# Cutting the first load of a DMA-bound loss kernel into halves on two queues

## The chip, the cores and the metric

The kernel runs on one core of a Trainium2 chip. The time is that of the whole program on the device in microseconds, the median of several executions. The profile is one execution; its span is some 1.8 us shorter than the time of the same run. All runs told of here were recorded as fast, at a granted clock of 1.0.

## The reference

Cross entropy with label smoothing over 256 rows of 32000 classes, in float32:

```python
def reference(logits, labels, smoothing):      # (256, 32000), (256,), 0.1
    log_probs = logits - np.max(logits, axis=-1, keepdims=True)
    log_probs = log_probs - np.log(np.sum(np.exp(log_probs), axis=-1, keepdims=True))
    smooth_targets = np.full((batch, num_classes), smoothing / num_classes)
    for i, label in enumerate(labels):
        smooth_targets[i, label] = 1.0 - smoothing + smoothing / num_classes
    return (-np.sum(smooth_targets * log_probs, axis=-1)).astype(np.float32)
```

Three things are needed of each row: the sum of the logits, the sum of their exponentials, and the one logit at the label. The logits are 32.77 MB, and each is read once.

## The kernel before

Each of the 128 partitions holds two rows. The first row comes in four loads of 8000 columns, the second in ten loads that shrink from 8000 to 832, so that little is left to do after the last byte. Wide loads share a ring of three buffers. VectorE sums the logits and ScalarE the exponentials, in pieces of up to 4000 columns.

```python
WIDTHS = (
    (8000, 8000, 8000, 8000),
    (8000, 6272, 4736, 3648, 2688, 2048, 1536, 1216, 1024, 832),
)
...
def _issue_first_transfers_at_start(nc):
    # the first DMA of the sync and of the scalar queue is moved ahead of the opening barrier
    main, body = nc.m.functions[0].blocks[:2]
    head, rest = list(main.instructions), list(body.instructions)
    for engine in (mybir.EngineType.SP, mybir.EngineType.Activation):
        at = next(i for i, ins in enumerate(rest)
                  if ins.engine == engine and ins.opcode == "DMACopy")
        ...
        head.insert(to, rest.pop(at))
...
    lab = small.tile([P, 2 * R], I32, name="lab", tag="lab")
    nc.scalar.dma_start(out=lab[:], in_=labels...)      # 16 bytes a partition
    ...  # GpSimd: flat_idx = row offset + label, then two gathers of logits[flat_idx] into gat
...
    def load(w, col, name):
        if w >= RING_MIN:
            xt = ring.tile([P, max(WIDTHS[0])], FP32, name="xt", tag="xt")
        else:
            xt = tail.tile([P, w], FP32, name=name, tag=name)
        nc.sync.dma_start(out=xt[:, :w], in_=x[:, col : col + w])
        return xt
```

The softmax here doesn't subtract the row's maximum and nothing guards it: scores larger than these inputs give would overflow.

## Time and profile before

| | before |
|---|---|
| time, median of 3 | 85.47 us (85.46 to 85.61) |
| span of the profiled run | 83.6 us |
| DMA, mean over the span | 392 GB/s |
| ScalarE busy, VectorE busy | 72%, 47% |
| labels, issue to landing | 12.2 us |

No engine is at its limit over the whole span, and yet the transfers run without a break from 1 us to 78.7 us. Read the chain of waits first, then the times at which each new tile is first used. The prediction below shows both. ("L181 ACT ja" is ScalarE's exponential, "L169 DVE jd" VectorE's sum; q1 is the sync queue, q10 the scalar queue, q0 the pool queue.)

### The profile page before, as it was taken

To read this page: it belongs to the slowest core of one execution; us is meant where nothing else is said; L and a number is where in the kernel's file an instruction comes from. 1 tells how busy PE (TensorE), PEld (TensorE's weight loads), DVE (VectorE), ACT (ScalarE), POOL (GpSimd) and SP (SyncE) were. 2 spreads that over 40 slices of the span, in tenths; PEclk is the share of its full clock that TensorE was granted. 3 is DMA by queue.
4 is the path that set the end of the run, shared out by engine and by line. 5 is a ranking of instruction groups with operands and counts; after the bars stand their busy time and mean duration, and the time that the engine had idled before them with its cause. 6 is when DMAs were issued, how large, how long until landed. Compare 5 with 4: busy or idle time off the path is not lost.

```text
span 83.6 us, 214 instructions
## 1 busy us (share of the span) xinstructions
PE 1.5 (2%) x4; PEld 0.3 (0%) x4; DVE 38.9 (47%) x52; ACT 59.9 (72%) x45; POOL 7.1 (8%) x13
## 2 busy tenths in 40 slices
PE   0000000000000000000001010000000000000030
PEld 0000000000000000000000000000000000000000
DVE  0000019900595009910497119923936654756760
ACT  5000019992699809994499909998999999999950
POOL 2000009981010000000000000000000000000000
DMA  8979998999899989999999999999999999999400
GB/s 245 414 322 490 460 429 352 475 460 429 353 475 429 444 368 475 460 414 398 444 475 429 398 397 456 432 420 399 426 412 433 430 412 424 411 412 406 179 4 0
DMA packets 2227, 32.78 MB, mean 392 GB/s; under 512 B 433, under 2 KB 434, under 8 KB 946
## 3 DMA queue, kind: packets, MB, share of 16 engines
q1 hardware_dynamic: 2018, 32.77, 92.5%
q10 hardware_dynamic: 144, 0.00, 0.1%
q0 software_dynamic: 64, 0.00, 0.1%
q14 instruction: 1, 0.01, 0.0%
HBM read 32.77 MB, written 0.00 MB: 392 GB/s over the span
## 4 chain that ended last, share of the span: by engine, by line
DMA 84%; ACT 9%; DVE 2%; issue 1%; PE 0%; SPq 0%; DVEq 0%; ACTq 0%
DMA xt<-in_logits_dram 59%; DMA xl<-in_logits_dram 26%; ACT ja L181 9%; DVE jd L169 1%; PE lin_t L191 0%; SPq L163 0%; DVE lin_row L193 0%; DVE res L196 0%; DVE done L270 0%; DVEq L196 0%; DVEq L270 0%; ACTq L181 0%
## 5 line engine op out<-in xcount | busy, mean ns | idle before, releaser
L181 ACT ACTIVATE ja<-xt 128x4000 bf16<-128x4000 f32 (+1 forms) x12 | 40.9, 3408 | 19.4 <-DMA xt<-in_logits_dram 19.4
L169 DVE SCALAR_TENSOR_TENSOR jd<-xt 128x2000 f32<-128x2000 f32 (+1 forms) x12 | 26.1, 2176 | 31.4 <-DMA xt<-in_logits_dram 31.2
L181 ACT ACTIVATE ja<-xl 128x2368 bf16<-128x2368 f32 (+7 forms) x9 | 16.5, 1839 | 0.0
L169 DVE SCALAR_TENSOR_TENSOR jd<-xl 128x1184 f32<-128x1184 f32 (+7 forms) x9 | 10.7, 1184 | 7.3 <-DMA xl<-in_logits_dram 7.1
L123 POOL DMA_INDIRECT gat<-in_logits_dram,flat_idx x2 | 3.9, 1938 | 0.5 <-issue 0.3
L115 POOL TENSOR_TENSOR flat_idx<-rowoff,lab 128x2 int32<-128x2 int32 x1 | 2.0, 1999 | 11.1 <-DMA lab<-in_labels_dram 11.1
L181 ACT ACTIVATION_READ_ACCUMULATOR ja<-xt 128x1 f32 x12 | 2.2, 186 | 0.0
L90 ACT ACT_TABLE_LOAD x1 | 1.3, 1283 | 0.9 <-PEq L293 0.9
L181 ACT ACTIVATION_READ_ACCUMULATOR ja<-xl 128x1 f32 x9 | 1.6, 182 | 0.0
L191 PE MATMUL lin_t<-ident,both 128*1 128x128 f32 x1 | 0.4, 373 | 45.7 <-DVE both L218 45.7
L146 POOL TENSOR_SCALAR xsum<-gat 128x1 f32<-128x1 f32 x2 | 0.4, 214 | 7.3 <-DMA gat<-in_logits_dram,flat_idx 7.3
L193 DVE COPY lin_row<-lin_t 1x128 f32<-1x128 f32 x2 | 0.6, 280 | 0.9 <-PE lin_t L191 0.9
L169 DVE DVE_READ_ACCUMULATOR jd<-xt 128x1 f32 x12 | 1.0, 81 | 0.0
L196 DVE SCALAR_TENSOR_TENSOR res<-lin_row,lse_t 1x128 f32<-1x128 f32 x2 | 0.6, 276 | 0.8 <-PE lse_t L195 0.7
L191 PE MATMUL lin_t<-ident,done 128*1 128x128 f32 x1 | 0.4, 373 | 31.5 <-DVE done L270 31.5
L221 DVE TENSOR_REDUCE both<-esum 128x1 f32<-128x8 f32 x1 | 0.2, 161 | 1.6 <-ACT ja L181 1.6
L195 PE MATMUL lse_t<-ident,lse 128*1 128x128 f32 x2 | 0.7, 373 | 2.4 <-ACT lse L187 2.4
L169 DVE DVE_READ_ACCUMULATOR jd<-xl 128x1 f32 x9 | 0.7, 82 | 0.0
L270 DVE TENSOR_TENSOR done<-done,pair 128x2 f32<-128x2 f32 x2 | 0.3, 160 | 0.2
L189 ACT ACTIVATE lse<-elast,done 128x1 f32<-128x1 f32 x1 | 0.3, 261 | 0.2 <-DVE done L270 0.2
L187 ACT ACTIVATE lse<-both 128x1 f32<-128x1 f32 x1 | 0.2, 203 | 0.2 <-DVE both L221 0.2
masks.py:199 POOL TENSOR_SCALAR_AFFINE_SELECT ident<-ident 128x128 f32<-128x128 f32 x1 | 0.3, 282 | 0.0
(12 smaller groups left out, 1.6 us busy)
## 6 DMA issues: line engine op xcount, KB each, us to landing
xt<-in_logits_dram SPq DMA_DIRECT2D x5, 4000.0 KB, 21.4
xt<-in_logits_dram SPq DMA_DIRECT2D x1, 3136.0 KB, 19.2
xl<-in_logits_dram SPq DMA_DIRECT2D x1, 2368.0 KB
xl<-in_logits_dram SPq DMA_DIRECT2D x1, 1824.0 KB, 28.3
xl<-in_logits_dram SPq DMA_DIRECT2D x1, 1344.0 KB, 31.1
xl<-in_logits_dram SPq DMA_DIRECT2D x1, 1024.0 KB, 33.1
xl<-in_logits_dram SPq DMA_DIRECT2D x1, 768.0 KB, 34.4
xl<-in_logits_dram SPq DMA_DIRECT2D x1, 608.0 KB, 35.4
```

The costliest lines, as they stand in the source:

```text
L90: nc.scalar.add_instruction(mybir.InstLoadActFuncSet(name=nc.get_next_instruction_name(), act_func_set_id=tbl, ins=[], outs=[],))
L115: nc.gpsimd.tensor_tensor(out=flat_idx[:], in0=rowoff[:], in1=lab[:].rearrange("p (r two) -> p r two", two=2)[:, :, 0:1], op=ALU.add,)
L123: nc.gpsimd.indirect_dma_start(out=gat[:, r : r + 1], out_offset=None, in_=logits[:], in_offset=bass.IndirectOffsetOnAxis(ap=flat_idx[:, r ...
L146: nc.gpsimd.tensor_scalar(out=xsum[:, 0:1], in0=gat[:, r : r + 1], scalar1=label_weight, scalar2=None, op0=ALU.mult,)
L169: return nc.vector.scalar_tensor_tensor(out=jd[:, :h], in0=xp[:, :h], scalar=1.0, in1=xp[:, h:w], op0=ALU.mult, op1=ALU.add, accum_out=out,)
L181: nc.scalar.activation(out=ja[:, :w], in_=xp, func=AF.Exp, accum_out=out)
L189: nc.scalar.activation(out=lse[:], in_=se, func=AF.Ln, bias=se_rest)
L191: nc.tensor.transpose(out=lin_t[:], in_=lin, identity=ident[:])
L193: nc.vector.tensor_copy(out=lin_row[:], in_=lin_t[:])
L195: nc.tensor.transpose(out=lse_t[:], in_=lse[:], identity=ident[:])
L196: nc.vector.scalar_tensor_tensor(out=res[:, :, r : r + 1], in0=lin_row[:], scalar=-c_small, in1=lse_t[:], op0=ALU.mult, op1=ALU.add,)
L270: nc.vector.tensor_tensor(out=done[i + 1][:], in0=done[i][:], in1=pairs[i][:], op=ALU.add)
```

## The change

The first load has nothing before it to hide behind. The change wants it to start on two queues at once, both ahead of the opening barrier (where the engines wait for one another at the start; the first issue behind it comes at 0.92 us in the kernel before). The labels held the scalar queue's place there, so they move to the pool queue, behind the barrier.

```diff
-    nc.scalar.dma_start(
+    nc.gpsimd.dma_start(
         out=lab[:], in_=labels.bitcast(I32).rearrange("(p f) -> p f", p=P)
     )
@@ load()
-        nc.sync.dma_start(out=xt[:, :w], in_=x[:, col : col + w])
+        if col == 0:
+
+            h = w // 2
+            nc.sync.dma_start(out=xt[:, :h], in_=x[:, :h])
+            nc.scalar.dma_start(out=xt[:, h:w], in_=x[:, h:w])
+        else:
+            nc.sync.dma_start(out=xt[:, :w], in_=x[:, col : col + w])
```

## The prediction

> **What bounds the kernel now.** I read the page's chain of work first, because an average over the span cannot say which wait ends last.
>
> ```profile
> ## 4 chain that ended last, share of the span: by engine, by line
> DMA 84%; ACT 9%; DVE 2%; issue 1%; PE 0%; SPq 0%; DVEq 0%; ACTq 0%
> q1 hardware_dynamic: 2018, 32.77, 92.5%
> ```
>
> The last line is the sync queue in the table of queues: packets, MB, share of the 16 DMA engines' span. The chain is a chain of transfers, and one queue carries all the logits. So the question is whether that stream ever stops. The timeline answers with the times at which the first operation on each new tile starts (start, length, engine; in brackets the idle time ahead and what ended it):
>
> ```profile
> 12.14 3.54 ACT L181 ACTIVATE ja<-xt 128x4000 bf16<-128x4000 f32 x1 [9.94 <-DMA xt<-in_logits_dram]
> ...
> 21.70 3.54 ACT L181 ACTIVATE ja<-xt 128x4000 bf16<-128x4000 f32 x1 [2.41 <-DMA xt<-in_logits_dram]
> ...
> 31.35 3.54 ACT L181 ACTIVATE ja<-xt 128x4000 bf16<-128x4000 f32 x1 [2.50 <-DMA xt<-in_logits_dram]
> ...
> 40.84 3.54 ACT L181 ACTIVATE ja<-xt 128x4000 bf16<-128x4000 f32 x1 [2.34 <-DMA xt<-in_logits_dram]
> ```
>
> A tile of 128 x 8000 floats is 4.096 MB. The tiles come 9.56 us apart (21.70 - 12.14), which is 4.096 MB / 9.56 us = 428 GB/s, and that pace doesn't change. ScalarE waits 2.3 to 2.5 us for each tile, so compute is not the bound here. Buffers aren't either: the fourth load is issued at 19.3 us, when the first tile has been used, while the queue still holds tiles two and three. From 57.7 us on ScalarE is busy without a gap (22.32 us of 22.40), fitted to the shrinking tiles, and the last tile lands as ScalarE is free for it. Both clocks hang on the same stream: move it by d and the end moves by about d.
>
> What is left to gain lies ahead of the stream. The first tile is used at 12.14 us; less 9.56 us of transfer, 2.58 us are fixed: issue, first byte, a ramp and the landing. Here is the ramp, by narrow windows of the DMA view (0 to 1.0, 1.0 to 2.5 and 2.5 to 12.2 us):
>
> ```profile
> DMA packets 0, 0.00 MB, mean 0 GB/s; under 512 B 0, under 2 KB 0, under 8 KB 0
> ...
> q1 hardware_dynamic: 16, 0.51, 113.7%
> ...
> q1 hardware_dynamic: 144, 4.10, 98.5%
> q10 hardware_dynamic: 144, 0.00, 0.8%
> ```
>
> No packet starts in the first microsecond. Then each of the 16 engines starts one packet of 32000 bytes (0.51 MB / 16), a whole row of the tile. Narrower windows put 12 of those starts before 1.3 us and the last four between 1.4 and 2.2 us. All 16 packets of that window take 1.137 x 1.5 us x 16 / 16 = 1.7 us each; from 5 to 6 us one takes 1.185 x 1.0 x 16 / 16 = 1.185 us. So the first packet costs 0.5 us more than a later one. After 2.5 us the labels' packets (q10, the scalar queue) stand beside those of the tile.
>
> **What the Trainium skill says.** "DMA: Bandwidth & Descriptors", section "Queues, rings and completion order": each DMA engine takes turns between the queues it has work for, packet by packet. The trace agrees: from 5 to 6 us both queues have 16 packets, one of 16 bytes for each of 32000. It explains a label load of 2 KB that takes 12.2 us from issue to landing (8 packets on each engine, each waiting for a 1.19 us row), and it says how two halves will share the engines.
>
> The same page, section "Issuing engines are not separate DMA queues": starting transfers from several engines saves only the sequencer's time of issue. In this trace that is short: the first issue on the sync queue takes 0.40 us, the label issue on the scalar queue runs from 0.12 for 0.38 us. Whether two queues fill the ramp better, the trace before can't show.
>
> The same page, section "Latency and other measured facts": first byte some 600 ns after a hardware-generated issue, some 1 us on the GpSimd path. The trace: issue done at 0.40 us, first packet at 1.00 us, so 0.6 us; no such row exists for a direct GpSimd load.
>
> The same page, section "Where 436 GB/s comes from": a ceiling of 435 GB/s at the ports. The stream's 428 GB/s is 98% of it, so a second queue has no rate to find.
>
> **The change, part by part.**
>
> 1. Labels leave the scalar queue. Removed: one issue of 0.38 us on a queue whose next work (the table load) waits for the barrier until 0.91 us anyway; worth 0. Also removed are 144 small packets among the first tile's rows, 0.8% of 9.7 us x 16 engines, which is 0.08 us an engine. They would come back on the pool queue in fewer packets: the two gathers, 256 elements and 32 completions by their shape, show only 64 packets there. I keep 0.06 us of gain.
>
> 2. Labels on the pool queue. Issued after the barrier, at about 1 us, landing at 3 to 6 us in place of 12.3, as grouped packets need fewer turns (my estimate). The index addition and the gathers then begin 6 to 9 us sooner. What needs them is the reduction over the label terms, at 45.48 us, while the second label term is ready at 26.79 us: 18.7 us of slack before, more after. Worth 0.
>
> 3. The first load in halves. Each half has 128 rows of 16000 bytes, so 8 packets an engine on either queue, turn by turn. The data is the same and so is its rate. What is added: 128 row packets more (the rows are cut in two) and 16 completions. For the cost of a packet I compare sizes. From 77.8 to 78.6 us, 63 packets take 51.6%, 6.60 us; less 15 completions of 9 ns, 48 rows of 3328 bytes take 0.135 us each. The line through (3328 B, 0.135 us) and (32000 B, 1.185 us) has a slope of 27.3 GB/s an engine and an offset of 0.013 us. Eight more packets an engine: 8 x 0.013 = +0.10 us.
>
> 4. The start. The sync issue at 0 us still has 128 rows to describe, so the first packet still comes at 1.00 us. The scalar queue's half is issued at 0.12 us, where the labels were, and its packets can be there from about 1.1 us. For twelve engines nothing is won. The four late ones start 0.4 to 1.1 us behind; if it is the sync queue's descriptors that they lack, the other queue may feed them sooner. The tile is complete only when the slowest engine is done. I give this 0.2 us: a third of the late engines' lag of 0.6 us, as the lag may equally be HBM answering late (the late packets are the shorter ones, and end only some 0.4 us behind the rest).
>
> 5. When compute may start. Each half carries its own completion, and the first piece of 4000 columns is just the first half. As the queues take turns, both end together near 12 us, so the first piece starts at most a packet or so earlier. ScalarE then waits 2.4 us for tile two anyway: worth 0.
>
> Sum: -0.06 + 0.10 - 0.2 = -0.16 us; 85.47 - 0.16 = 85.31, which I round to 85.3 us.
>
> **The rivals.**
>
> Nothing moves at all. The late starts are HBM's, and the packet costs cancel: 85.4 to 85.5 us. For it: the late packets are short. Against it: little; it is nearly as likely as my own.
>
> The start is won in full. All engines begin at 1.0 us and the doubled supply hides part of the first packet's extra 0.5 us: 0.5 to 0.8 us less, 84.7 to 85.0 us. For it: 2.58 us are fixed, and two queues give an engine two packets to work on at once. Against it: the engine already had a queue of packets behind the first, and still showed the 0.5 us.
>
> The second half comes late. If the scalar queue starts later or is served less, the sync queue goes on with tile two, and the first tile is whole some time after 12.14 us. For it: nothing, as the labels got one turn in two. Against it: ScalarE's idle 2.4 us ahead of tile two takes up such a delay, and bytes are only reordered: within 0.1 us of 85.47.
>
> A new cost elsewhere. The pool load could hold up the barrier or slow the stream. Against it: it is issued after the barrier, and the gathers on the same queue passed beside the stream between 16 and 20 us without a change of the 9.56 us step. If wrong, 85.6 to 85.8 us.
>
> **Range and chances.** Most outcomes lie from the full start (84.9) to a small new cost (85.7); the runs before spread over 0.15 us. Two per cent are 1.71 us. To gain that, two thirds of the fixed 2.58 us would have to go; to lose it, the stream would have to stop for longer than a row's packet takes. I see no row for either: 2% each, and 96% for within 2%.
>
> **What would show each step.** Right: DMA packets start at about 1.0 us and carry 16000 bytes on both queues, in equal number, up to about 12 us; tile two is used 0 to 0.4 us before 21.70, and every later tile and the end by as much; the label load lands before 7 us and the gathers run before 12; the steps between tiles stay at 9.56 us. Step 4 is wrong if the first packets are as staggered as before, or if tile two comes more than 0.5 us sooner. Step 3 is wrong if tile two comes later than 21.70 us with the same start. The whole account is wrong if the steps between tiles change, if ScalarE waits for anything but a landing or its own work, or if the end moves by an amount other than tile two's.

## The result, and the profile after

| | before | after |
|---|---|---|
| time, median of 6 | 85.5 us (85.38 to 85.66) | 85.3 us (85.15 to 85.46) |
| ratio, 95% interval | | 0.9975 [0.9957, 0.9993] |
| span of the profiled run | 83.6 us | 83.5 us |

A ratio is the mean time of one kernel's fast runs over that of the other's in the same rounds, so not quite the ratio of the medians. The gain is 0.0025 x 85.5 = 0.21 us, with an interval of 0.06 to 0.37 us. It is clear of zero and small. The two profiled runs took 85.36 us (before) and 85.33 us (after), so they differ by far less than the gain.

The chain of waits after. Its tail now runs through ScalarE where it ran through the transfers:

```profile
## 4 chain that ended last, share of the span: by engine, by line
DMA 59%; ACT 34%; DVE 2%; issue 1%; PE 0%; SPq 0%; DVEq 0%; ACTq 0%
```

This is no new bottleneck. In both kernels ScalarE works without a gap from the first use of tile six on (57.77 us before, 57.70 us after), the last tiles land just about when it is free for them, and from there to the issue of the result the two take 23.63 and 23.68 us. The chain's share moves by 25 points while that stretch changes by 0.05 us.

The timeline after, with the first operation on each half of tile one and on tiles two to four (start, length, idle time ahead):

```profile
11.50 3.54 ACT L187 ACTIVATE ja<-xt 128x4000 bf16<-128x4000 f32 x1 [9.31 <-DMA xt<-in_logits_dram]
...
15.04 3.52 ACT L187 ACTIVATE ja<-xt 128x4000 bf16<-128x4000 f32 x1
...
21.73 3.54 ACT L187 ACTIVATE ja<-xt 128x4000 bf16<-128x4000 f32 x1 [3.07 <-DMA xt<-in_logits_dram]
...
31.27 3.54 ACT L187 ACTIVATE ja<-xt 128x4000 bf16<-128x4000 f32 x1 [2.40 <-DMA xt<-in_logits_dram]
...
40.76 3.54 ACT L187 ACTIVATE ja<-xt 128x4000 bf16<-128x4000 f32 x1 [2.33 <-DMA xt<-in_logits_dram]
```

Tile one is used 0.64 us sooner than before (11.50 against 12.14), but tile two comes at 21.73 in place of 21.70, tile three at 31.27 in place of 31.35. ScalarE spends the head start waiting: 3.07 us ahead of tile two, where it was 2.41. The result's transfer is issued at 81.38 us in place of 81.40. So this pair of profiles shows 0.02 us of the 0.21 at the end, and at most 0.08 on the way; the rest lies in how the runs spread.

The DMA issues after (KB, us from issue to landing):

```profile
xt<-in_logits_dram SPq DMA_DIRECT2D x1, 2000.0 KB, 11.5
xt<-in_logits_dram ACTq DMA_DIRECT2D x1, 2000.0 KB, 13.1
...
lab<-in_labels_dram POOLq DMA_DIRECT2D x1, 2.0 KB, 6.5
```

The halves don't land together: the scalar queue's, issued at 0.12 us, lands near 13.2 us, 1.7 us after the sync queue's. The first microseconds show when they start. ("Ramp" means here the stretch from the first packet until every engine keeps the steady pace.) The DMA view of the changed kernel from 1.0 to 2.8 us and from 2.8 to 3.0 us:

```profile
q1 hardware_dynamic: 32, 0.51, 98.4%
...
q10 hardware_dynamic: 9, 0.14, 172.1%
```

Before 2.8 us the scalar queue moves nothing. The sync queue's first 32 packets, two on each engine, are the same 0.51 MB that the kernel before moved as 16 whole rows by then. Only after them do the queues take turns. The second queue thus gave the ramp no byte more.

### The profile page after: what moved, and what is told of

Read it like the earlier page. It is cut to its first block, busy times and chain, and to the rows that moved or that the text cites. A ratio compares the mean times of both kernels' runs of the same rounds, so it can differ in the third digit from the quotient of the medians.

```text
span 83.5 us, 217 instructions
## 1 busy us (share of the span) xinstructions
PE 1.5 (2%) x4; PEld 0.3 (0%) x4; DVE 38.7 (46%) x52; ACT 59.9 (72%) x45; POOL 4.2 (5%) x14
## 4 chain that ended last, share of the span: by engine, by line
DMA 59%; ACT 34%; DVE 2%; issue 1%; PE 0%; SPq 0%; DVEq 0%; ACTq 0%
DMA xt<-in_logits_dram 59%; ACT ja L187 34%; DVE jd L175 1%; PE lin_t L197 0%; DVE done L276 0%; SPq L169 0%; DVE lin_row L199 0%; DVE res L202 0%; ACTq L187 0%; DVEq L202 0%; DVEq L276 0%
## 5 line engine op out<-in xcount | busy, mean ns | idle before, releaser
L123 POOL DMA_INDIRECT gat<-in_logits_dram,flat_idx x2 | 2.0, 1002 | 0.7 <-POOL ident masks.py:199 0.4
L103 POOL DMA_DIRECT2D lab<-in_labels_dram x1 | 0.8, 753 | 1.0 <-POOLq L299 1.0
L115 POOL TENSOR_TENSOR flat_idx<-rowoff,lab 128x2 int32<-128x2 int32 x1 | 0.2, 195 | 5.4 <-DMA lab<-in_labels_dram 5.4
## 6 DMA issues: line engine op xcount, KB each, us to landing
xt<-in_logits_dram SPq DMA_DIRECT2D x1, 2000.0 KB, 11.5
```

Source lines behind the costliest of these rows:

```text
L103: nc.gpsimd.dma_start(out=lab[:], in_=labels.bitcast(I32).rearrange("(p f) -> p f", p=P))
L123: nc.gpsimd.indirect_dma_start(out=gat[:, r : r + 1], out_offset=None, in_=logits[:], in_offset=bass.IndirectOffsetOnAxis(ap=flat_idx[:, r ...
```

## The experiments

Each kernel was run beside the kernel before on the same chip. All gave correct results. The first four shared one set of 11 runs of before (median 85.51 us), the next four one of 7 (85.34 us), the last four one of 11 (85.41 us). My theory was the prediction's sum: packets cost, the second queue's ramp gains. The first rival was that the labels' move is all of it, the second that nothing moves.

**The changed kernel once more.** No edit.

> The changed kernel once more, as the measure for the other three of this call. Theory (the prediction's sum): 0.16 us less than the kernel before, ratio 0.998. Rival (nothing moves): ratio 1.000 within 0.001. The profile should repeat what the first one showed: the first half used near 11.5 us, the second landing near 13.2 us, tile two used within 0.1 us of the 21.70 us of before.

Measured: 85.33 us, ratio 0.9969 [0.9935, 1.0003]. Tile one used at 11.56, tile two at 21.80, the scalar half landing 13.2 us after its issue. The wider interval comes from before, which ranged from 85.23 to 86.21 us, while the changed kernel stayed within 85.25 to 85.39. With the first result the gain is now measured twice at 0.2 to 0.3 us, though this second interval just reaches zero gain.

**Labels only.** The first load whole on the sync queue, nothing of the scalar queue ahead of the barrier:

```diff
-    for engine in (mybir.EngineType.SP, mybir.EngineType.Activation):
+    for engine in (mybir.EngineType.SP,):
-            nc.sync.dma_start(out=xt[:, :h], in_=x[:, :h])
-            nc.scalar.dma_start(out=xt[:, h:w], in_=x[:, h:w])
+            nc.sync.dma_start(out=xt[:, :w], in_=x[:, :w])
```

> Only the labels move to the pool queue; the first load stays whole on the sync queue. The prediction's sum gives this part -0.06 us, ratio 0.9993. Rival (all of the measured 0.2 us comes from taking the label packets out of the first tile's rows and the gathers to another time): ratio 0.9975, like the whole change. If the split is what gains, this one stays at 0.999 to 1.000.

> Labels on the pool queue and the first load whole, once more, as the intervals of the first four runs overlap. Prediction's sum: 0.9993. Labels are all of it: 0.9975 or lower, and below the split-only kernel of this call by 0.002.

Measured: 85.39 us, ratio 0.9978 [0.994, 1.0016]; and later 85.35 us, 0.9990 [0.9969, 1.0011]. Both intervals hold both expectations. The two profiles of this one kernel are worth more than its times. Tile two and the issue of the result, first in the profile of a run of 85.67 us:

```profile
22.17 3.54 ACT L185 ACTIVATE ja<-xt 128x4000 bf16<-128x4000 f32 x1 [2.72 <-DMA xt<-in_logits_dram]
...
81.81 0.32 SPq L278 DMA_DIRECT2D out_dram<-res  x1
```

then tile two in the profile of a run of 85.36 us:

```profile
21.91 3.54 ACT L185 ACTIVATE ja<-xt 128x4000 bf16<-128x4000 f32 x1 [2.54 <-DMA xt<-in_logits_dram]
```

The same program has tile two 0.26 us apart in two runs that are 0.31 us apart. They come from two chips, but on the first of them alone this kernel ranged from 85.17 to 85.74 us. Such differences in the first 20 us are as large as the whole effect, so no single pair of profiles can account for 0.2 us.

**Split only.** The labels stay on the scalar queue, behind the half; the half is the one that goes ahead of the barrier:

```diff
-    nc.gpsimd.dma_start(
+    nc.scalar.dma_start(
         out=lab[:], in_=labels...
-        at = next(
+        found = [
             i for i, ins in enumerate(rest)
             if ins.engine == engine and ins.opcode == "DMACopy"
-        )
+        ]
+        at = found[1 if engine == mybir.EngineType.Activation else 0]
```

> Only the split: halves on the sync and the scalar queue ahead of the barrier, the labels on the scalar queue behind the half. The prediction's sum gives +0.10 for the packets and -0.2 for the ramp, -0.10 us, ratio 0.9988. Rival (labels are all of it): ratio 1.000 or a little above (up to 1.001, for eight more packets an engine).

> Halves on two queues with the labels behind the half on the scalar queue, once more. Prediction's sum: 0.9988. Labels are all of it: 1.000 to 1.001, above the labels-only kernel of this call by 0.002.

Measured: 85.52 us, ratio 0.9994 [0.9957, 1.0031]; later 85.35 us, 0.9996 [0.9974, 1.0017]. Again both intervals hold both expectations, and the two parts differ by 0.0006 later, where "labels are all of it" asked for 0.002. The means of the two calls are 0.9984 for labels only, 0.9995 for split only and, with its first result, 0.9972 for the whole change. They lean towards the labels, but the difference of 0.0011 is 0.1 us, and each interval reaches 0.0021 or more to either side: the order of the two parts is not settled.

**Both halves on the sync queue.** The packets of the change, without its second queue. The second half is issued behind the barrier, at 0.80 us:

```diff
-    for engine in (mybir.EngineType.SP, mybir.EngineType.Activation):
+    for engine in (mybir.EngineType.SP,):
-            nc.scalar.dma_start(out=xt[:, h:w], in_=x[:, h:w])
+            nc.sync.dma_start(out=xt[:, h:w], in_=x[:, h:w])
```

> Both halves on the sync queue, the first ahead of the barrier, the second behind it; labels on the pool queue. It has the packets of the change without its second queue. The prediction's sum gives -0.06 + 0.10 = +0.04 us, ratio 1.0005. If the second queue is worth nothing (the changed profile shows its first packet only at 2.8 us, behind two packets of the sync queue), this one ties with the whole change, ratio 0.9975, and the first half is used some 5 us sooner, near 7.5 us, with no effect on the end.

> Both halves on the sync queue, labels on the pool queue, once more: it was the fastest of the first four. If the second queue gains nothing, again 0.996 to 0.998, no slower than the changed kernel's 0.9975; by the prediction's step 4 it should lack the 0.2 us of the ramp and stand at 1.0005.

Measured: 85.25 us, ratio 0.9963 [0.993, 0.9997]; later 85.22 us, 0.9985 [0.9959, 1.0011]. It is as fast as the changed kernel, with the lowest median. The later interval holds 1.0005 too, so by time it is the first that speaks: there the six runs of the changed kernel average 85.33 us and the six of this one 85.25, where step 4 had the second queue 0.2 us ahead. Its first profile: the DMA view from 1.0 to 2.8 us, then the first uses of the two halves and of tile two.

```profile
q1 hardware_dynamic: 33, 0.53, 101.4%
```

```profile
7.50 3.54 ACT L187 ACTIVATE ja<-xt 128x4000 bf16<-128x4000 f32 x1 [5.42 <-DMA xt<-in_logits_dram]
...
12.08 3.54 ACT L187 ACTIVATE ja<-xt 128x4000 bf16<-128x4000 f32 x1 [0.95 <-DMA xt<-in_logits_dram]
...
21.71 3.54 ACT L187 ACTIVATE ja<-xt 128x4000 bf16<-128x4000 f32 x1 [5.99 <-DMA xt<-in_logits_dram]
```

33 packets on one queue, where the two queues had 32 (all of them of the sync queue): the ramp is the same. The first half comes 4 us sooner than with two queues, and nothing comes of it: ScalarE waits 5.99 us for tile two, which is there at 21.71. The claim that the second queue gains 0.2 us in the ramp falls with this.

**The start behind the barrier.** This asks whether the end follows the stream at all:

```diff
-    nc.at_finalize(_issue_first_transfers_at_start)
```

> The changed kernel with both halves issued behind the opening barrier. Central claim (move the stream by d and the end moves by d): the first packet comes some 0.8 us later, at 1.8 us, tile two and the end by as much, so +0.6 us over before, ratio 1.007. If the end hangs on something else (ScalarE's tail), ratio under 1.002.

Measured: 86.29 us, ratio 1.0104 [1.0083, 1.0125]. From its timeline, the first issues, then tile two and the issue of the result:

```profile
0.73 0.40 SPq L165 DMA_DIRECT2D xt<-in_logits_dram  x1
0.76 0.39 ACTq L166 DMA_DIRECT2D xt<-in_logits_dram  x1
...
22.86 3.54 ACT L186 ACTIVATE ja<-xt 128x4000 bf16<-128x4000 f32 x1 [2.79 <-DMA xt<-in_logits_dram]
...
82.50 0.32 SPq L279 DMA_DIRECT2D out_dram<-res  x1
```

Against the changed kernel, tile two is 1.13 us later (22.86 - 21.73) and the result's issue 1.12 us (82.50 - 81.38). The end follows the stream one to one, as claimed. The size was off: the issue is 0.73 us later, as is the first packet (1.75 us in place of 1.0), and 0.4 us more is lost before tile two. Part of that can be chance, as the labels-only kernel showed; I have no run that splits it. One thing is different here: the scalar queue's packets start at 2.5 us, 1.3 us after its issue ends, and both halves land within 0.1 us of each other (0.73 + 12.2 and 0.76 + 12.3).

**The first tile on the scalar queue.** Why was that queue late? Here it is alone ahead of the barrier:

```diff
-    for engine in (mybir.EngineType.SP, mybir.EngineType.Activation):
+    for engine in (mybir.EngineType.Activation,):
-            nc.sync.dma_start(out=xt[:, :h], in_=x[:, :h])
-            nc.scalar.dma_start(out=xt[:, h:w], in_=x[:, h:w])
+            nc.scalar.dma_start(out=xt[:, :w], in_=x[:, :w])
```

> The first tile whole on the scalar queue ahead of the barrier, nothing of the sync queue ahead of it. Asks why the scalar queue's packets came only at 2.8 us. If that queue starts late by itself, its first packet stands near 2.6 us again, the sync queue's tile two goes first from some 1.7 us. If it was only behind the two packets that each engine had taken from the sync queue, its first packet stands near 1.0 us. Tile one then shares its turns with tile two and is used late, at 18 to 20 us; ScalarE has about 20 us to spare over the span but waits in the middle, so the time may rise by up to 3 us, ratio 1.00 to 1.04.

The DMA view from 0 to 1.4, from 1.4 to 5.0 and from 5.0 to 6.0 us:

```profile
q10 hardware_dynamic: 9, 0.29, 71.2%
...
q10 hardware_dynamic: 39, 1.25, 86.3%
...
q1 hardware_dynamic: 15, 0.28, 66.5%
```

Alone, the scalar queue starts between 1.0 and 1.2 us, as promptly as the sync queue did: it isn't late by itself. Now it is the sync queue that comes late: its first load is issued from 0.93 to 1.33 us and moves nothing until after 5 us, while each engine takes three rows from the scalar queue. So in both runs the queue that reached the idle engines first kept them to itself, for 1.8 us in the change and 4.1 us here. That settles which queue waits; why the wait lasts so long, no run shows. The time, 90.84 us (ratio 1.0647, beyond the 1.04 expected), says nothing on this: the program builder put one of the later, smaller loads (4736 columns) first on the sync queue, so the order of the loads differs.

**Rows cut in quarters.** The cost of a cut row, made large: the four other loads of 8000 columns come as four loads of 2000 each.

```diff
-            nc.sync.dma_start(out=xt[:, :w], in_=x[:, col : col + w])
+            q = w // 4 if w == max(WIDTHS[0]) else w
+            for o in range(0, w, q):
+                nc.sync.dma_start(out=xt[:, o : o + q], in_=x[:, col + o : col + o + q])
```

> The changed kernel with the other four loads of 8000 columns cut into quarters on the sync queue: 24 more row packets an engine for each of four tiles, 96 in all. The prediction's 0.013 us a packet gives +1.25 us over the changed kernel, so +1.05 us over before, ratio 1.012, and a step between tiles of 9.87 us in place of 9.56. If a cut row costs nothing beside its neighbours: as the changed kernel, ratio 0.9975, step 9.56.

Measured: 86.01 us, ratio 1.0080 [1.0063, 1.0097]. From its timeline, the second piece of tile two and of tile five:

```profile
26.74 3.54 ACT L191 ACTIVATE ja<-xt 128x4000 bf16<-128x4000 f32 x1 [1.15 <-DMA xt<-in_logits_dram]
...
50.93 3.54 ACT L191 ACTIVATE ja<-xt 128x4000 bf16<-128x4000 f32 x1 [1.20 <-DMA xt<-in_logits_dram]
```

ScalarE takes two pieces of a tile, and waits for a landing before each of the six from the first of these lines to the last: five half tiles, 24.19 us, 9.68 us a tile. With whole rows the steps from tile three to tile five in the changed kernel were (50.24 - 31.27) / 2 = 9.49 us. The 24 packets and three completions added cost 0.19 us, 7 ns each. By time: (1.0080 - 0.9972) x 85.34 = 0.92 us over 108 packets and completions, 8.5 ns each, or 6 to 11 ns with the intervals of both ratios (my estimate; the two come from different calls). The prediction's 13 ns, taken from a line through two packet sizes, was too much.

**Nine label loads.** The cost of small packets, made large: eight more loads of the labels behind the first in the kernel before, into tiles that nothing reads.

```diff
+    for j in range(8):
+        more = small.tile([P, 2 * R], I32, name=f"more{j}", tag=f"more{j}")
+        nc.scalar.dma_start(out=more[:], in_=labels...)
```

> The kernel before with eight more label loads on the scalar queue, into tiles that nothing reads: the cost of one label load beside the rows, times eight. The prediction's 0.08 us an engine for one load gives +0.64 us, ratio 1.0075. Rival (the label packets are all of the 0.2 us that the change gained, each turn costs more than its own 9 ns): +1.6 us, ratio 1.019. If small packets cost the stream nothing: ratio 1.000.

Measured: 88.62 us, ratio 1.0391 [1.0368, 1.0414], beyond every expectation. The waits of the sync queue name the cause:

```profile
SPq L168 <- DMA more<-in_labels_dram: 11.7, 1, 11.7
```

A logits load waited 11.7 us for one of the added label loads, with which it shares no data. The trace says why: its entry for each issue, which the views don't print, names the semaphore that the transfer counts up when it lands and the one that the issue waits for. In this run the loads on the sync and scalar queues take eight semaphores in turn, numbers 100 to 107. The second logits load has number 102, which the first added label load had before it; that one landed at 12.54 us, and the logits load was issued at 12.56. In the 40 slices of this run the rate falls to 6 GB/s at 10.8 us. The experiment shows what a starved stream costs, not what small packets cost.

**One transfer of small packets.** The same question with one more load, 64 runs of 16 bytes on each engine:

```diff
+    more = small.tile([P, 8, 8], FP32, name="more", tag="more")
+    nc.scalar.dma_start(
+        out=more[:, :, 0:4],
+        in_=x[:, 0:64].rearrange("p (j k) -> p j k", k=8)[:, :, 0:4],
+    )
```

> The eight extra label loads stopped the stream for another reason than their packets (the second logits load waited for one of them to land, a semaphore being used again), so the cost of small packets is asked again with one transfer: the kernel before with one more load on the scalar queue, 64 runs of 16 bytes an engine, into a tile that nothing reads. At the 9 ns that the trace shows for one, 64 x 9 ns = +0.58 us, ratio 1.007. Rival (the nine packets an engine of one label load are all of the 0.2 us gained, some 22 ns each): +1.4 us, ratio 1.017. If they cost nothing: 1.000.

Measured: 88.88 us, ratio 1.0401 [1.0373, 1.0428]. One waiting load spoiled this time too, but only near the end: the load of 2688 columns has the semaphore of the added load, which landed at 68.79 us, and was issued at 68.81. The sync queue's waits, and the rate in 40 slices of 2.2 us:

```profile
SPq L168 <- DMA more<-in_logits_dram: 28.5, 1, 28.5
```

```profile
GB/s 235 397 353 427 456 442 456 427 383 427 427 471 412 383 427 456 442 456 398 383 442 442 430 369 473 439 404 418 400 410 370 20 252 433 431 400 419 264 4 4
```

The hole is at slice 32 (67 to 70 us). Ahead of it the stretch is clean. From tile two to tile six every engine moves 32 rows, each with one small packet beside it, as the DMA view from 25 to 30 us shows (the first two lines are the kernel with the added load, the last is before):

```profile
q1 hardware_dynamic: 64, 2.05, 95.3%
q10 hardware_dynamic: 65, 0.00, 0.7%
```

```profile
q1 hardware_dynamic: 64, 2.05, 95.1%
```

Tile two to tile six take 58.54 - 22.15 = 36.39 us here and 57.77 - 21.70 = 36.07 us in the kernel before: 0.32 us for 32 small packets, 10 ns each. One label load, nine packets an engine, therefore costs 0.09 us. The rival that gives all of the gain to these packets, at 22 ns each, falls.

## Why the prediction was right

The predicted time was 85.3 us and the measured one is 85.3; the predicted change -0.16 us, the measured -0.21 with 0.06 to 0.37 as its interval. The frame held, but not all the terms.

- **The stream sets the end.** Right, and shown: with the start behind the barrier, a tile two later by 1.13 us gave an end later by 1.12. Two halves or one, an earlier first tile is worth nothing (7.50, 11.50 or 12.14 us, all with tile two near 21.7).
- **The step of 9.56 us "doesn't change".** Not quite: in the kernel before the steps between tiles are 9.56, 9.65 and 9.49 us. The slowest holds the gathers' packets, which run from 21.0 to 26.1 us and not, as the prediction read it, between 16 and 20 us, when only their instructions ran; after the change the packets run sooner and that step is 9.54.
- **Step 1, labels off the scalar queue.** Right in size: 0.08 us by its own working, 0.09 us by the added small packets. The set-off of 0.02 us for the pool queue was never timed by itself, but its packet count fits: that queue moves 96 packets after the change and 64 before, two more an engine.
- **Step 2, labels on the pool queue.** Worth nothing, as said. Its time was not: used at 8.07 us, where 3 to 6 us was the estimate and 7 us the mark. Its issue ends at 2.19 us and no packet of its queue starts before 5.8 us. Whether this is the wait behind another queue that the scalar queue met too, no run shows.
- **Step 3, cut rows.** The right sign, too large: 7 to 8.5 ns a packet, so 0.06 to 0.07 us in place of +0.10.
- **Step 4, the ramp.** This step failed. "Its packets can be there from about 1.1 us" is contradicted by the profile, which has none before 2.8 us, and the 0.2 us it was to gain can't come from there: on one queue the same halves give the same ramp and the same time. The trace before had the warning in it: the label load, issued at the same 0.12 us on the same queue, has no packet before 2.6 us (a window from 0 to 2.6 us shows q1 alone), and the prediction's own view from 1.0 to 2.5 us shows none of q10. (Also, of the four late first packets three are short; the one of 1.6 to 1.8 us took 1.79 us, more than the average of 1.7.)
- **Step 5, compute.** Worth 0, as said, for half of the reason. The halves don't end together near 12 us; they end at 11.5 and 13.2. The first half keeps ScalarE busy to 15.04 us, which hides it. The rival "the second half comes late" was right in its event; its time, within 0.1 us of 85.47, can't be told from the measured one.

So the total came out right by luck, with its largest term wrong. Without step 4, and with the measured sizes, steps 1 and 3 cancel (-0.09 + 0.02 + 0.07). What then carries the measured 0.21 us isn't settled. The two parts lean to -0.14 us for the labels and -0.04 for the split (0.0016 and 0.0005 of 85.5), each with 0.18 us or more to either side.

The profiles do show where runs differ. In the ten profiles of before, of the change, of its parts and of the start behind the barrier, the stretch from the first use of tile six to the issue of the result takes 23.63 to 23.70 us, whatever the kernel, so the end is settled by the time at which tile six is whole. Here is the first use of tile six in the slow-starting profile of labels only (a run of 85.67 us; its result was issued at 81.81), then that use and the issue of the result with both halves on the sync queue (a run of 85.18 us):

```profile
58.16 2.82 ACT L185 ACTIVATE ja<-xt 128x3136 bf16<-128x3136 f32 x1 [0.32 <-DMA xt<-in_logits_dram]
```

```profile
57.69 2.82 ACT L187 ACTIVATE ja<-xt 128x3136 bf16<-128x3136 f32 x1 [0.30 <-DMA xt<-in_logits_dram]
...
81.37 0.32 SPq L280 DMA_DIRECT2D out_dram<-res  x1
```

A load is whole when the last of the 16 engines has completed its share, and the trace has these completions one by one (the views print only the last). The first engine is done with tile six at 56.99 us in the one run and 56.98 in the other; the last engine at 58.08 and 57.61. This lag between first and last engine is there at tile two already (1.08 and 0.60 us) and is much the same at the last tile (1.06 and 0.61). So in this run some engine fell behind before tile two, and the lag stayed to the end. Averaged over the engines, the last tile is complete between 78.75 and 78.91 us in all nine profiles with the start ahead of the barrier, with before the earliest: nothing shows that the change made the stream itself shorter. The last engine comes 0.36, 0.69 and 0.28 us after that average in the three profiles with the first load whole, and 0.23 to 0.36 us in the six with it cut. The gain may lie there, but three profiles against six don't show it; it would take many more.

## What to carry to other kernels

When a stream without gaps sets the end, count what moves the whole stream; a first tile that lands sooner, by 0.6 us or by 4.6, is worth nothing if the second tile stays where it was. A second queue onto the same busy engines is not a second start: look at which packets move in the first microseconds before giving it a gain; a small load that already sits on that queue shows when its packets start. Each tile here was as late as the last of its 16 engines. And before you explain 0.2 us, compare two profiles of the same kernel; here they differed by 0.26 us at tile two.

## What the Trainium skill lacked or had wrong

- "DMA: Bandwidth & Descriptors", section "Queues, rings and completion order", says that an engine takes turns between the queues it has work for. The runs agree once both queues are going (16 packets each from 5 to 6 us before the change), but the page lacks how long a second queue takes to join in: first packet just after 2.8 us, 2.4 us after its issue ended (the change); over 3.5 us after (the sync queue behind the scalar queue's load); 0.6 us after where the engines were idle.
- The same page, section "Latency and other measured facts", gives some 1 us to the first byte on the GpSimd path. Beside a full stream the label load on that path took 3.6 us from the end of its issue (2.19 us) to its first packet (after 5.8 us).
- The same page, section "Bandwidth", has a price per packet for a small transfer on its own. No page that I looked up has the price of a small packet beside a full stream, which these runs put at 10 ns for one of 16 bytes and 7 to 8.5 ns for each further cut of a row.
- No page that I looked up says that a load can wait for another transfer with which it shares no data; here it did so for 11.7 and 28.5 us, because both counted on one of eight completion semaphores that are used in turn, and each time the stream then ran dry and the run was over 3 us longer.
